# The value projection by seven products, and the order of the linear-attention layer around it

## Chip, cores, metric

The kernel runs on one core of one Trainium2 chip. The metric is device time in microseconds (us) of one execution. Before the change it is 1091.93 us, the median of three runs (1091.86 to 1092.0).

## The reference

Two residual layers over 512 tokens of width 1024: first bidirectional gated linear attention, then softmax attention, each followed by a gated feed-forward block with a width-3 convolution. Only the first half of layer 0 changes here:

```python
def gla_mixer(h, w_in, w_gate_up_f, b_gate_f, w_gate_up_b, b_gate_b, norm_w, w_out):
    proj = h @ w_in
    q, k, v, g, r = jnp.split(proj, ...)
    r_f, r_b = jnp.split(r, 2, axis=-1)
    def log_decay(r_dir, w_up, b_up):
        return heads(jax.nn.log_sigmoid(r_dir @ w_up + b_up) / 16.0, GLA_DK)
    ...
    o_f = gla_chunked(q, k, v, la_f, strict=False)
    o_b = flip(gla_chunked(flip(q), flip(k), flip(v), flip(la_b), strict=True))
    o = rmsnorm((o_f + o_b).transpose(0, 2, 1, 3), norm_w) * jax.nn.silu(g)
    return o.reshape(B, S, GLA_VAL_DIM) @ w_out

x = x + gla_mixer(rmsnorm(x, norm_mix[0]), ...)
```

There are 4 heads with keys of 128 and values of 256; q and k are 512 wide, v and g 1024, r 32. All is float32.

## The kernel before

**Numbers and products.** TensorE takes float32 in a rounded form (`F32R`). Each operand is therefore kept as a high part, the rounded value, and a low part, what the rounding left; a product is three matmuls: high by high, high by low, low by high (`mm3`). A weight tile of 128x1024 is loaded by SP (`raw`), rounded on ScalarE (`wh`) and subtracted on VectorE (`wl`); this is a split (`Weights.split`, L301 to L310). `Weights.low_dma` (L260) makes the low part in another way: ScalarE writes the high part, then the negated high part, and an accumulating DMA on POOL's queue adds the original (`flush`, L298). `Weights` holds a list `todo` of all weight halves in the order of their use, makes them some pieces ahead and asks for loads `LOADS` = 3 ahead. The program's order is a priority: where an instruction isn't ready by the planner's costs, a later one of the same engine is put ahead of it, except where `tc.issue_after` ties it.

**The stage, in order (`gla`).** The tokens are 512, the width is 8 chunks `k` of 128.

1. The input comes as eight 512 KB pieces `xw`, each a chunk of x and the same chunk of the first weights. `norm.chunk` makes `xhl`, the weighted input in two parts.
2. `seg(0)`, `seg(1)` (`token_steps`, L488): v, each half of 512 columns in 4 token blocks x 8 chunks x 3 = 96 matmuls of 128x512. `seg_out` scales a half by the token's inverse norm (`rtok`) and splits it.
3. Beside them: the sums of squares (`norm.square`, L443; `norm.tokens`, `norm.rows`), the rank step `rp` (16 matmuls, L668), its weights and those of the gates, the masks, and `token_sums`, which makes sums of quarters of the input (`xt`) for step 4.
4. `seg_seven`: g by Strassen's scheme in Winograd's form. Tokens, columns and chunks are halved; seven products take the place of eight, each 24 matmuls per half of the weights and product. It needs sums of weight quarters (`make_vg`, four VectorE operations for each of two halves) and the token sums. The seven products are added up in PSUM and in SBUF (L616 to L627).
5. The gates (`gate`, eight: head x direction): a matmul `z`, then absolute value, clamp, exponential, logarithm, a scan over tokens within chunks of 64, and exponentials into `ek` and `fk`. They are begun at set points (`GATE_STEPS`, `LATE_GATES`).
6. Four heads. For each: `kproj`, `qproj` (a key and a query tile, 24 matmuls each), `keys` and `factors` (products with `ek`), `rows` (transposed keys, `kt`, split), `inner` (masked scores `in`; `masked` makes `ath`, `atl`), `outer` (eighteen state matmuls `kv` and twelve on `o`), `outputs` (twelve more on `o` with the states `sa`, `sb`), `gated` (per-token root, times g after silu, copied by DMA into `gr`), `tail` (transposes into `oT`). The projections of the next head stand between the steps of a head.
7. `out_steps`: the output projection, 192 matmuls `op`, added to x, and the next norm's chunks.

The feed-forward of layer 0 follows with the matmuls `up`.

Of the kernel before, what the change touches and what calls it, by code (L numbers as in the profile page):

```python
# [14 lines left out]
P = 128  # L15
# [11 lines left out]
SEG_BANKS = (("acc", "acc", "pt", "pt"), ("s", "s", "acc", "acc"), ("acc", "pt", "pt", "s"), ("s", "acc", "acc", "acc"))  # L27


KQ_DMA = 4  # L30
KQ_AHEAD = 2
BIG_GATES = 9
GATED = 0
WARM = 10
LATE_GATES = {0: (4,), 10: (4,), 30: (4, 5), 40: (5,), 1: (5, 6), 11: (6,), 21: (6,), 31: (7,), 41: (7,), 2: (7,)}
GST_LOW = 0
SEVEN_BANKS = (("pt", "pt"), ("acc", "acc"), ("acc", "s"))
GATE_STEPS = (2, 5, 18, 19, 99, 99, 99, 99)
GATE_LAG = 1
VG_ORDER = (1, 7, 6, 4, 5, 2, 3)  # L40
VG_AHEAD = 3
VG_RAW = {1: (4, "g"), 7: (5, "raw"), 6: (6, "raw"), 2: (7, "raw")}
VG_DMA = ()
SUMS_FIRST = 2
SUMS_AT = {1: 3}
SUMS_MID = (2,)
SUMS_OUT = ()
# [47 lines left out]
def hybrid_encoder_kernel(  # L95
# [9 lines left out]
    w_vg: bass.AP,  # L105
# [50 lines left out]
    def x_save(p):  # L156
        if p == 0:
# [10 lines left out]
    class Weights:  # L168
# [9 lines left out]
        def add(self, src, strips=None, pieces=2):  # L178
            for i in strips or range(src.shape[0]):
# [4 lines left out]
        def load_vg(self, i, half):  # L184
            if i not in VG_RAW or (i, half) in self.vg:
                return
            strip, tag = VG_RAW[i]
            self.vg[i, half] = t = big(F32, "raw") if tag == "g" else pair("raw", NR, F32, "raw")
            sync.dma_start(t, w_vg[strip, :, half * 2 * S : (half + 1) * 2 * S])

        def make_vg(self, i, half):

            self.load_vg(i, half)
            a11, a21, a22, a12 = (self.vg.get((n, half)) for n in (1, 7, 6, 2))
            r = {1: a11, 6: a11, 4: a22, 5: a21, 2: a12, 3: a12}.get(i)
# [9 lines left out]
            if i in VG_DMA:  # L205
                strip = {1: 4, 4: 6, 2: 7}[i]
                self.low_dma(hi, lo, r, w_vg[strip, :, half * 2 * S : (half + 1) * 2 * S].bitcast(F32R))
            else:
                self.split(hi, lo, r)
            return hi, lo  # L210
# [12 lines left out]
        def load(self, key):  # L223
            src, i, h = key
            if i < 0:
                self.load_vg(-i, h)
# [8 lines left out]
        def make(self, key):  # L235
            src, i, h = key
            if i < 0:
                self.made[id(src), i, h] = self.make_vg(-i, h)
# [11 lines left out]
            else:  # L250
                self.split(hi, lo, r, 2 if src is w_vg and i < 2 else 1, src is w_vg and i == 0 and h == 0)
# [99 lines left out]
    W.add(w_vg, range(4))  # L351
    W.todo += [(w_vg, -i, half) for i in VG_ORDER for half in range(2)]
    for a in (w_kq, w_gout):
        W.add(a)
# [16 lines left out]
    for n in range(4):  # L371
        W.loaded[id(w_vg), n // 2, n % 2] = [t[:, S:] for t in raw[2 * n : 2 * n + 2]]
# [115 lines left out]
    def token_steps(src, i0, hl, ps, width, per_half):  # L488

        for hf in range(KC // per_half):  # L490
            wh, wl = W.half(src, i0 + hf)

            late = src is w_vg and i0 > 0 and hf == 0
            for kk in range(per_half):
                todo = [(kk, j, i) for j in range(NT - late) for i in range(3)]
                if late and kk == 1:
                    todo += [(k, NT - 1, i) for k in range(2) for i in range(3)]
                if src is w_vg and i0 + hf * per_half + kk < 2:
                    todo.sort(key=lambda a: a[2])
# [12 lines left out]
    def out_steps(src, hl, nxt, late):  # L512
# [4 lines left out]
        def part(ng, ks):  # L517
            if ng not in pss:
                pss[ng] = [bank("s" if ng % 2 else "acc", "op") for _ in range(2)]
            for k in ks:  # L520
# [4 lines left out]
                for i, (wt, mv) in enumerate(((wh, hl[k][0]), (wh, hl[k][1]), (wl, hl[k][0]))):  # L525
                    for n in range(2):
                        sl = slice((kk * 2 + n) * P, (kk * 2 + n + 1) * P)
                        mm(pss[ng][n], wt[:, sl], mv, start=k == 0 and i == 0, stop=k == KC - 1 and i == 2)  # L528
# [3 lines left out]
        def end(ng):  # L532
# [4 lines left out]
            x_save(ng)  # L537

        for ks in late:
            for ng in range(2):  # L540
                yield from part(ng, ks)
                if KC - 1 in ks:
                    end(ng)
        for ng in (2, 3):
            yield from part(ng, range(KC))
# [3 lines left out]
    def gla(norm, nxt):  # L549
# [7 lines left out]
        v = [(big(F32R, "vh"), None) for _ in range(NT)]  # L557
        q = []

        def seg(i, between=None):  # L560
            ps = [bank(tag, "vg") for tag in SEG_BANKS[i]]
            for n, _ in enumerate(token_steps(w_vg, i * 4, norm.hl, ps, S, 2)):
                if between is not None:
                    between(n)
            return ps

        def seg_out(ps, h):
            for j in range(NT):
                if h == 0:
                    v[j] = v[j][0], pair("x", KC // 2, F32R, "vl")  # L570
                hi, lo = (a[:, h * S : (h + 1) * S] for a in v[j])
                r = norm.rtok[:, j : j + 1]
                act.activation(hi, ps[j], AF.Copy, scale=r)
                dve.scalar_tensor_tensor(lo, ps[j], r, hi.bitcast(F32), ALU.mult, ALU.subtract)
# [984 lines left out]
```

## Time and profile before

| | |
|---|---|
| median of 3 runs | 1091.93 us |
| the profiled execution | 1092.29 us |
| its span, first to last instruction | 1090.6 us |
| granted TensorE clock, mean | 0.999 |
| first matmul of `vg` / first of `up` | 5.84 / 223.75 us |
| HBM read, written | 114.89, 14.68 MB |

In the profile, PE is TensorE, PEld its weight loads, DVE is VectorE, ACT ScalarE, POOL GpSimd, SP the engine whose queue carries the loads. A row of the grouped view reads: line, engine, operation, output<-inputs by the program's names, shapes, count | busy us, mean ns of one | idle time before them and what ended it. A row of the view by stretches has the stretch, its length, then for each engine the busy us and the instructions, the granted clock, the DMA share and GB/s. A row of the timeline has start, length, engine, line, output<-inputs and count. A wait row reads: engine, what waited <- what it waited for: us in total, times, longest. A DMA row ends with the median time from issue to landing. The end of a matmul is modelled; matmuls overlap.

### The profile page before, as it was taken

The page shows a single profiled execution, that of the slowest core. Times are in us where ns is not written, and L with a number is a line of the kernel's source. Part 1 is how long each engine was busy: PE and PEld are TensorE (multiplying, and loading weights), DVE is VectorE, ACT ScalarE, POOL GpSimd, SP SyncE. Part 2 cuts the span into 40 slices and gives each one's busy share as a digit, 9 for nine tenths or more (in the row PEclk, how much of TensorE's full clock was granted, in tenths as well). Part 3 has the DMA queues.
Part 4 walks back from the last instruction along what each step waited for, and adds up shares of the span by engine and source line. Part 5 has one row for each costly group of instructions (what it writes and reads, how often), then busy time and mean ns, then how long its engine had stood idle before and what let it go on. Part 6 is the DMA issues. An engine that isn't in the chain of part 4 may idle for free.

```text
span 1090.6 us, 17422 instructions
## 1 busy us (share of the span) xinstructions
PE 1083.5 (99%) x6696; PEld 971.1 (89%) x6696; DVE 873.4 (80%) x1304; ACT 715.9 (66%) x1120; POOL 136.1 (12%) x153
## 2 busy tenths in 40 slices
PE   9999999999999999999999999999999999999998
PEld 8878888888899999999988888788889999999997
DVE  6886784659898899988855588765989889998882
ACT  8768753469775676666664677646977567665660
POOL 0101222021000100010014343002110010001000
PEclk9999999999999999999999999999999999999999
DMA  9537624488644733265757475558964373226542
GB/s 308 138 116 192 156 97 155 154 186 204 151 117 120 166 115 101 80 158 133 264 131 168 121 215 151 168 173 189 212 138 139 99 167 111 99 87 158 132 174 78
DMA packets 55187, 164.26 MB, mean 151 GB/s; under 512 B 6464, under 2 KB 6976, under 8 KB 55104
## 3 DMA queue, kind: packets, MB, share of 16 engines
q1 hardware_dynamic: 36192, 112.66, 31.3%
q0 software_dynamic: 14016, 41.95, 21.3%
q10 hardware_dynamic: 4896, 8.55, 2.1%
q8 instruction: 52, 0.85, 0.3%
q14 instruction: 31, 0.25, 0.1%
HBM read 114.89 MB, written 14.68 MB: 119 GB/s over the span
## 4 chain that ended last, share of the span: by engine, by line
PE 94%; ACT 3%; DVE 2%; issue 1%; DMA 1%; DVEq 0%; ACTq 0%; SPq 0%
PE r L1035 39%; PE op L528 8%; PE up L470 6%; PE up L471 6%; PE up L472 6%; PE vg L502 3%; PE dn L471 2%; PE dn L470 2%; PE dn L472 2%; PE vg L610 2%; PE av L502 1%; PE o L876 1%; PE A L470 1%; PE A L472 1%; PE B L472 1%; PE B L470 1%
## 5 line engine op out<-in xcount | busy, mean ns | idle before, releaser
L309 ACT ACTIVATE wh<-raw 128x1024 fp32r<-128x1024 f32 x144 | 149.7, 1052 | 73.3 <-PE op L528 22.7
L310 DVE TENSOR_TENSOR wl<-raw,wh 128x1024 fp32r<-128x1024 f32 x144 | 175.2, 1220 | 27.4 <-ACT wh L309 27.2
L1035 PE MATMUL r<-gu,wh 128*128 128x256 f32 x896 | 161.2, 282 | 0.0
L1035 PE MATMUL r<-xt,wh 128*128 128x256 f32 x832 | 150.9, 282 | 0.0
L1035 PEld LDWEIGHTS r<-gu,wh 128*128 128x128 f32 x896 | 139.4, 190 | 1.0 <-ACT r L1172 0.2
L1035 PEld LDWEIGHTS r<-xt,wh 128*128 128x128 f32 x832 | 129.3, 190 | 1.0 <-ACT r L1056 0.5
L1035 PE MATMUL r<-gu,wl 128*128 128x256 f32 x448 | 126.3, 283 | 0.0
L1035 PE MATMUL r<-xt,wl 128*128 128x256 f32 x416 | 117.2, 283 | 0.0
L1035 PE MATMUL r<-nh,wh 128*128 128x256 f32 x312 | 88.7, 284 | 0.0
L1035 PE MATMUL r<-nh,wl 128*128 128x256 f32 x312 | 88.2, 283 | 0.0
L1035 PE MATMUL r<-nl,wh 128*128 128x256 f32 x312 | 87.9, 282 | 0.0
L1035 PEld LDWEIGHTS r<-gu,wl 128*128 128x128 f32 x448 | 85.1, 190 | 0.0
L1035 PEld LDWEIGHTS r<-xt,wl 128*128 128x128 f32 x416 | 79.0, 190 | 0.0
L470 PE MATMUL up<-nh,wh 128*128 128x512 f32 x192 | 75.3, 392 | 0.0
L471 PE MATMUL up<-nl,wh 128*128 128x512 f32 x192 | 75.3, 392 | 0.0
L472 PE MATMUL up<-nh,wl 128*128 128x512 f32 x192 | 75.2, 392 | 0.0
L528 PE MATMUL op<-oT,wh 128*128 128x512 f32 x256 | 71.8, 394 | 0.0
L261 ACT ACTIVATE wh<-raw 128x1024 fp32r<-128x1024 f32 x40 | 42.2, 1055 | 37.0 <-PE up L471 12.1
L1035 PEld LDWEIGHTS r<-nh,wh 128*128 128x128 f32 x312 | 59.3, 190 | 2.5 <-ACT r L1063 2.2
L1035 PEld LDWEIGHTS r<-nl,wh 128*128 128x128 f32 x312 | 59.4, 190 | 0.2
L1035 PEld LDWEIGHTS r<-nh,wl 128*128 128x128 f32 x312 | 59.4, 190 | 0.0
L310 DVE TENSOR_TENSOR wl<-sum,wh 128x1024 fp32r<-128x1024 f32 x44 | 53.6, 1220 | 4.4 <-ACT wh L309 4.4
(290 smaller groups left out, 2768.6 us busy)
## 6 DMA issues: line engine op xcount, KB each, us to landing
raw<-in_w_up_dram SPq DMA_DIRECT2D x84, 512.0 KB, 4.6
raw<-in_w_down_dram SPq DMA_DIRECT2D x44, 512.0 KB, 3.6
wl<-raw POOLq DMA_DIRECT2D x24, 512.0 KB, 5.1
wl<-in_w_up_dram POOLq DMA_DIRECT2D x16, 512.0 KB, 7.7
ring<-p ACTq DMA_DIRECT2D x32, 256.0 KB, 2.8
raw<-in_w_vg_dram SPq DMA_DIRECT2D x12, 512.0 KB, 5.9
xw<-in_xw_dram SPq DMA_DIRECT2D x8, 512.0 KB, 7.0
raw<-in_w_kq_dram SPq DMA_DIRECT2D x8, 512.0 KB, 4.6
```

The source lines that it names most:

```text
L261: act.activation(hi, r, AF.Copy)
L309: act.activation(hi[:, sl], a, AF.Copy)
L310: dve.tensor_tensor(lo[:, sl], a, hi[:, sl].bitcast(F32), ALU.subtract)
L470: mm(ps, wh, mh, start=start, stop=False)
L471: mm(ps, wh, ml, start=False, stop=False)
L472: return mm(ps, wl, mh, start=False, stop=stop)
L502: mm(ps[j][:, :width], hl[k][i == 2][:, j * P : (j + 1) * P], (wl if i == 1 else wh)[:, sl], start=k == 0 and i == 0, stop=k == KC - 1 and ...
L528: mm(pss[ng][n], wt[:, sl], mv, start=k == 0 and i == 0, stop=k == KC - 1 and i == 2)
L610: mm(ps[j], m[:, js], w[:, sl], start=i in (1, 7, 2) and p == 0 and a == 0, stop=i in (4, 2, 3) and p == 3 and a == 2, skip_group_check=True)
L876: last = mm(og[s], l, r, start=False, stop=i == len(parts) - 1, skip_group_check=True)
L1035: mm(dst, w[:, sl], m, start=start and j == 0 and a == 0, stop=j == len(pairs) - 1 and a == 2, skip_group_check=True)
```

## The change

**Order.** The four key/query tiles of heads 0 and 1 take the place of v's first half: they are computed beside the arriving input (`first_tiles`, with the weights as the stationary operand), since `xw` now carries their weights. Then come the key and query of head 2 (`more`, one step of a tile at a time), with rank step and norm beside them, then v by seven products, then the heads; the two tiles of head 3 stand ahead of head 0 and inside head 1 (`FILL_AT`). g by seven products comes behind all heads, the output projection behind g.

**Heads.** `rows` and `inner` of the next head stand ahead of `outputs` of this one. `outputs` copies `o` to SBUF (`O`, two ScalarE copies a head); the squares and roots (`roots`) come in g's stage, and `gated` works on one token block and one half of the columns at a time, as soon as that quarter of g is done. The tails of heads 2 and 3 stand in g's last products, those of heads 0 and 1 behind eight steps of the output projection, which now begins with chunks 4 to 7.

**Weights and sums.** The seven products use another choice of signs, in which every sum of weights is a plain addition; one of four is an accumulating DMA. The token sums of three of four pairs are scaled on VectorE, and three of four low parts are made there. v's quarters need an intermediate tile (`part`), then a high copy and a low difference.

**Gates.** The clamp moves from VectorE to ScalarE (a relu of the negated input) and the addition to an accumulating DMA on POOL's queue.

`PLAN` names the point at which each of these small pieces is issued: f, s, e, v, g for the steps of the first tiles, of head 2's tiles, of head 3's, of v and of g, h for places in the heads.

```diff
-KQ_DMA = 4
-BIG_GATES = 9
-SEVEN_BANKS = (("pt", "pt"), ("acc", "acc"), ("acc", "s"))
+FIRST_BANKS = (("acc", "acc", "pt", "pt"), ("s", "s"))
+SEVEN_BANKS = {"v": (("acc", "acc"), ("pt", "pt"), ("s", "s")), "g": (("acc", "acc"), ("pt", "pt"), ("acc", "po"))}
+BIG_GATES = 4
+MORE = 2
+KQ_DMA = 3
+VG_SUMS = (5,)
+SUM_DMA = (0,)
+SUM_DVE = (0,1,2)
+PLAN = {"f0": ("q5", "q3", "q2", "A1", "s0", "w", "P", "q7", "q4",), "f1": ("q6",), "f2": ("q1",), "f3": ("q0", "s1",), "f4": ("s2", "T",), "f5": ("R",), "f6": ("M",), "first": ("k0", "k2",), "s1": ("k3", "g",), "s6": ("k1", "r",), "s12": ("z1", "s3",), "s13": ("E",), "v1": ("z0",), "v3": ("z1",), "v5": ("z1",), "v6": ("z0",), "v7": ("K0",), "v8": ("z2",), "v13": ("F0", "z3",), "e0": ("z0",), "e4": ("z4", "K1",), "e5": ("z5",), "h0a": ("z4",), "h0b": ("z3", "z5", "z4",), "h0c": ("z3",), "e8": ("z2",), "e15": ("z7", "z2",), "h0d": ("z7",), "h1a": ("K2", "K3", "F1",), "h2a": ("z5", "z6", "z6",), "h3d": ("z6",), "g1": ("S1",), "g2": ("S0",), "g4": ("S3",), "g6": ("S2",), "g11": ("z7",)}
+FILL_AT = (-1,1)
+OUT_FIRST = 8
+TAILS = {"g11": 2, "g12": 3}
...
-            if i == 7:
-                r = pair("raw", NR, F32, "sum")
-                dve.tensor_tensor(r, a21, a11, ALU.subtract)
-            elif i == 6:
-                dve.tensor_tensor(a21, a21, a22, ALU.subtract)
-                dve.tensor_tensor(a11, a11, a21, ALU.subtract)
-            elif i == 3:
-                dve.tensor_tensor(a12, a12, a11, ALU.subtract)
+            plus = {7: a21, 6: a22, 5: a22, 3: a11}.get(i)
+            if plus is not None and i not in VG_SUMS:
+                dve.tensor_tensor(r, r, plus, ALU.add)
...
+            if i in (7, 2) and {7: 5, 2: 3}[i] in VG_SUMS:
+                r, plus = (a21, a22) if i == 7 else (a12, a11)
+                ...
+                self.pending.append((r, plus))
...
+        def more(n, tag):
+            h, i = 2 + n // 2, n % 2
+            ps = bank(tag, "kq")
+            for step, last in enumerate(feature_steps(*W.half(w_kq, n, KQ_AHEAD), norm.hl, ps)):
+                yield last
+            kq_out(h, i, ps)
...
+                if p in SUM_DVE:
+                    dve.tensor_scalar(y[:, i * S : (i + 1) * S], x[2 * p + i], norm.weight(2 * p + i), None, ALU.mult)
+                else:
+                    act.activation(y[:, i * S : (i + 1) * S], x[2 * p + i], AF.Copy, scale=norm.weight(2 * p + i))
...
+            if p in SUM_DMA:
+                W.low_dma(hi, lo, y)
+            else:
+                act.activation(hi, y, AF.Copy)
+                dve.tensor_tensor(lo, y, hi.bitcast(F32), ALU.subtract)
...
-            dve.tensor_scalar(m, z, b, 0.0, ALU.add, ALU.min)
+            act.activation(m, z, AF.Relu, bias=nb, scale=-1.0)
             act.activation(a, a, AF.Exp, scale=-1.0)
             act.activation(a, a, AF.Ln, bias=1.0)
-            dve.tensor_tensor(m, m, a, ALU.subtract)
+            pool.dma_start(m, a, accum_op=ALU.add)
...
+            O[h] = big(F32, "o")
+            for s in (2, 0):
+                act.activation(O[h][:, s * DV : (s + 2) * DV], og[s], AF.Copy)
...
+        def gated(c, o):
+            act.activation(g[c][:, o], g[c][:, o], AF.Silu)
+            for h in ((0, 1) if o.start == 0 else (2, 3)):
+                ...
+                dve.scalar_tensor_tensor(r, O[h][:, cs], ORS[h][:, c : c + 1], r, ALU.mult, ALU.mult)
+                pool.dma_start(gr[h][:, cs].bitcast(F32), r)
...
+        def v_done(c, o):
+            act.activation(v[c][0][:, o], v_part(c, o), AF.Copy)
+            dve.tensor_tensor(v[c][1][:, o], v_part(c, o), v[c][0][:, o].bitcast(F32), ALU.subtract)
...
+        last = seg_seven(w_v, "v", v_part, v_done, v_last)
+        if 0 not in fronts:
+            last = rows(0, last)
+        banks, last = inner(0, last)
+        at = masked(banks)
+        if -1 in FILL_AT:
+            last = fill()
         for h in range(GH):
+            tick(f"h{h}a")
+            st, og, last = outer(h, at, last)
+            tick(f"h{h}b")
+            if h + 1 < GH:
+                keys(h + 1)
+                last = rows(h + 1, last)
+                banks, last = inner(h + 1, last)
+                at = masked(banks)
+            tick(f"h{h}c")
+            if h in FILL_AT:
+                last = fill()
+            last = outputs(h, st, og, last)
+            tick(f"h{h}d")
+        g = [big(F32, "g") for _ in range(NT)]
...
+        seg_seven(w_g, "g", lambda c, o: g[c][:, o], gated, g_last)
...
+        osteps = out_steps(w_gout, oh, nxt, ((4, 5, 6, 7), (0, 1), (2, 3)), (1, 0))
+        for i in range(OUT_FIRST):
             next(osteps)
         sync.dma_start(cw, conv)
+        tail(0)
+        tail(1)
```

The layout of the weights follows: the first two heads' key and query columns go with the input, v and g are each stored as four quarters. `rows(0, last)` also stands inside `seg_seven` at v's step 12 (`ROWS_AT`).

More of the change, by code (lines that the diff above doesn't have):

```diff
@@ L491, in token_steps @@
             wh, wl = W.half(src, i0 + hf)
-            late = src is w_vg and i0 > 0 and hf == 0
             for kk in range(per_half):
[L495 to L499, printed above, removed]
+                todo = [(kk, j, i) for j in range(NT) for i in range(3)]
                 for a, j, i in todo:
@@ L510, in token_tiles, with out_steps @@
             pass
-    def out_steps(src, hl, nxt, late):
+    def out_steps(src, hl, nxt, late, order=(0, 1)):
         pss, ws = {}, {}
@@ L578, in token_sums, with whole @@
+        def whole(steps):
+            for res in steps:
+                pass
+            return res
         def token_sums(p):
@@ L961, in gla @@
-        last = outputs(GH - 1, st, og, last)
-        gated(GH - 1, og)
+        actions = {"q": norm.square, "s": token_sums, "T": lambda _: norm.tokens(), "R": lambda _: norm.rows(),
+                   "w": rank_weights, "g": gate_weights, "P": ranks, "r": rank_rows, "M": masks, "E": table,
+                   "k": lambda n: kq_out(n // 2, n % 2, made["kq"][n]), "z": lambda n: next(gates[n], None),
+                   "K": keys, "F": factors, "S": roots, "A": W.ahead}
+        made["kq"] = first_tiles()
```

483 lines of the change are left out of this document (220 added, 263 removed).

## The prediction

> **What bounds the kernel now.** The page comes first: its span and the line of TensorE.
>
> ```profile
> span 1090.6 us, 17422 instructions
> PE 1083.5 (99%) x6696; PEld 971.1 (89%) x6696; DVE 873.4 (80%) x1304; ACT 715.9 (66%) x1120; POOL 136.1 (12%) x153
> ```
>
> TensorE (PE) is busy for 99% of the span, so a matmul taken out shortens the kernel unless a wait takes its place. The changed stage is the gated linear attention, up to the first up-projection. I cut it at the first matmul of each part: the front (v and g), of it the seven products of g, then the heads, then the output projection.
>
> ```profile
> core 0: us, PE busy (x) PEld busy (x) DVE busy (x) ACT busy (x) POOL busy (x), PEclk, DMA share, GB/s
> 5.84:95.80 89.96, 89.28 (x394) 72.88 (x393) 74.95 (x109) 68.70 (x97) 7.07 (x9) 1.00 0.60 181
> ...
> 55.60:95.80 40.20, 39.52 (x172) 31.67 (x170) 34.12 (x41) 27.15 (x37) 1.72 (x2) 1.00 0.45 131
> 95.80:175.62 79.82, 79.24 (x458) 69.22 (x457) 59.71 (x107) 52.00 (x103) 20.41 (x26) 1.00 0.49 133
> 175.62:223.75 48.13, 48.10 (x223) 39.60 (x221) 24.21 (x37) 19.57 (x33) 5.84 (x10) 1.00 0.53 175
> ```
>
> The granted clock is 1.00 throughout. VectorE (DVE) comes second: 74.95 us busy in the 89.96 us of the front (83%), then 75% in the heads. The waits of TensorE up to 260 us are three:
>
> ```profile
> PE warm L386 <- DVE bd L392: 1.3, 1, 1.3
> PE vg L610 <- DVE wl L310: 0.6, 1, 0.6
> PE o L865 <- DVE atl L828: 0.4, 2, 0.3
> ```
>
> Waits can also hide in matmuls whose modelled ends cover them, so I count starts, not ends. The next rows give the rank step, and the group it belongs to:
>
> ```profile
> 28.30 3.79 PE L668 MATMUL rp<-xhl,rw 128*128 128x512 f32 x16
> 31.92 0.39 PE L502 MATMUL vg<-wh,xhl 128*128 128x512 f32 x1
> ...
> L668 PE MATMUL rp<-xhl,rw 128*128 128x512 f32 x16 | 3.8, 389 | 0.0
> ```
>
> Sixteen matmuls of 512 columns hold TensorE from 28.30 to 31.92, which is 3.62 / 16 = 0.226 us each, although the profile calls one 389 ns long. The price of such a matmul in a full queue is 0.226.
>
> **The matmuls.** These rows count what computes v (L502) and g (L610):
>
> ```profile
> L502 PE MATMUL vg<-wh,xhl 128*128 128x512 f32 x128 | 40.0, 397 | 0.0
> L502 PE MATMUL vg<-wl,xhl 128*128 128x512 f32 x64 | 24.0, 390 | 0.0
> L610 PE MATMUL vg<-wh,xt 128*128 128x512 f32 x64 | 20.2, 392 | 0.0
> L610 PE MATMUL vg<-wh,xhl 128*128 128x512 f32 x48 | 15.4, 389 | 0.0
> L610 PE MATMUL vg<-wl,xt 128*128 128x512 f32 x32 | 12.8, 399 | 0.7 <-DVE wl L310 0.6
> L610 PE MATMUL vg<-wl,xhl 128*128 128x512 f32 x24 | 9.3, 389 | 0.0
> ```
>
> v takes 192, g by seven products 64 + 48 + 32 + 24 = 168. With v by seven too, 24 go: 24 x 0.226 = 5.42 us. The key and query tiles (192 matmuls), rank step, gates, transposes, states and output projection keep their counts; they only move. This is the main term: **-5.4 us**.
>
> [...]
>
> **The new stage lengths.** The front (up to the end of v) loses 96 matmuls of v's second half's plain form against 48 of head 2's two tiles, since v's 168 stand where g's stood: 89.96 - 48 x 0.226 = 79.1 us, and 0.7 for head 0's transposes makes 79.8, with the stalls of before in it. The heads lose the six key/query tiles that now stand ahead of v: 79.82 - 144 x 0.226 - 0.7 = 46.6. The new block of g is 168 x 0.226 = 38.0; the output projection stays 48.1. So VectorE and ScalarE get 10 us less in the front and 33 less in the heads. Whether they keep up decides what is left of the 5.4.
>
> **VectorE in the front.** The durations:
>
> ```profile
> L310 DVE TENSOR_TENSOR wl<-raw,wh 128x1024 fp32r<-128x1024 f32 x26 | 31.5, 1221 | 10.4 <-ACT wh L309 10.4
> L698 DVE TENSOR_TENSOR gm<-gm,ga 128x512 f32<-128x512 f32 x8 | 6.8, 844 | 5.4 <-ACT ga L697 5.3
> L695 DVE TENSOR_SCALAR gm<-z,prm 128x512 f32<-128x512 f32 x8 | 6.0, 747 | 2.2 <-ACT ga L694 1.9
> L627 DVE SCALAR_TENSOR_TENSOR g<-vg,rtok,g 128x512 f32<-128x512 f32 x6 | 4.2, 746 | 0.1
> L802 DVE TENSOR_TENSOR ktl<-kt,kth 128x384 fp32r<-128x384 f32 x8 | 4.2, 546 | 0.0
> L828 DVE TENSOR_TENSOR atl<-at,ath 128x512 fp32r<-128x512 f32 x4 | 2.8, 691 | 0.0
> L890 DVE SCALAR_TENSOR_TENSOR g<-o,ors,g 128x256 f32<-128x256 f32 x16 | 6.6, 478 | 3.5 <-POOL ors L404 3.5
> ```
>
> and, from another part of the kernel, the nearest row of a scaled copy between buffers:
>
> ```profile
> L1389 DVE TENSOR_SCALAR p<-p,rc x32: 471/478/2282, 610.5 to 701.1; 128x512 f32<-128x512 f32 x32
> ```
>
> What goes: four splits of v's plain second half (4 x 1.22 = 4.9); two of eight weight sums of the same 128x1024 form (2.4), since one of four per half of the weights becomes an accumulating DMA; the clamps and additions of the four gates begun there, now ScalarE's and the DMA's (4 x 0.75 + 3 x 0.84 = 5.5), and a third gate's scan and fixing (1.9, by a 1.22 scan and half-width rows near 0.42). Evacuation: eight products of v at 0.75 and seven of g at 0.75 become six accumulations (0.746), six low halves (0.69) and two last ones (0.75): -1.1. Together -15.8. What comes: six scalings of keys and queries (6 x 0.69 = 4.1); six scaled copies for the token sums, a form that before shows on this engine only as L1389 (6 x 0.48 = 2.9; bounds 0.48 and, by L695, 0.75); three low halves of those sums that were DMAs (3 x 1.22 = 3.7); head 0's keys and factors (4 x 0.70) and transposed low halves (2 x 0.55), 3.9. Together +14.6. VectorE's 74.95 becomes 73.8 of 79.8 us, or **92%**, up from 83%.
>
> I cost this at nothing because of a stretch of the feed-forward behind:
>
> ```profile
> 240.00:285.00 45.00, 45.00 (x199) 37.06 (x198) 44.52 (x77) 41.62 (x53) 9.62 (x11) 1.00 0.88 192
> ```
>
> VectorE is busy 44.52 of 45.00 there, and TensorE 45.00. ScalarE loses six scalings, three low halves and four splits and gains the gates' clamps, so it stays near its 76% (68.70 of 89.96). The cover is thin all the same. The first product with token sums of g shows it at 61 to 72 us, where starts slip by 1.6 us: 40.20 for 168 x 0.226 = 38.0 and two gate matmuls (0.45); the wait of 0.6 on `wl` above is part of it. There are two such sets now. v's meets a fuller VectorE, g's comes behind the heads with loads and sums in hand. Each can cost 0 to 1.7; I take 2.1 for both, **+0.5** on before.
>
> **The heads.** Their VectorE work of 59.71 us loses, by the same rows and the counts in that window, six scalings (4.1), head 0's part (3.9), the gating of three heads (12 x 0.48 = 5.8), four splits of output weights (4.9), four clamps and five additions of gates (7.2), a fifth gate's scan (1.9) and four tail halves (4 x 0.75 = 3.0): 30.8. It gains g's first four splits and two sums (7.3) and v's last parts (4.4): 40.6 of 46.6, or 87%. Throughput suffices. What is exposed is the chain behind the masked scores: copy, predicated copy, high half, low half, then `o`. Two of the four heads have no projection tile behind it any more. Before shows one head with a tile behind its inner products:
>
> ```profile
> 128.23 1.95 PE L815 MATMUL in<-ek 128*128 128x128 f32 x16
> 129.93 0.48 PE L470 MATMUL k<-xhl,wh 128*128 128x512 f32 x1
> ```
>
> ```profile
> 137.88 0.69 DVE L828 TENSOR_TENSOR atl<-at,ath 128x512 fp32r<-128x512 f32 x1
> ```
>
> and the last head, which has none, from the `outputs` of the head before (L876) to its own first products (L865):
>
> ```profile
> 167.48 0.60 PE L876 MATMUL o<-sb,ek 128*128 128x256 f32 x2
> ...
> 170.07 1.95 PE L815 MATMUL in<-ek 128*128 128x128 f32 x16
> 171.78 0.36 PE L470 MATMUL kv<-vh,kth 128*128 128x256 f32 x1
> ...
> 173.98 0.28 PE L865 MATMUL o<-vh,ath 128*128 128x256 f32 x1
> ...
> 174.22 0.28 PE L865 MATMUL o<-vh,ath 128*128 128x256 f32 x1
> 174.45 0.39 PE L865 MATMUL o<-vh,atl 128*128 128x256 f32 x1
> ```
>
> In the bare head the product with `atl` starts 0.23 behind its neighbour instead of 0.12 (half of 173.98 to 174.22): a slip of 0.1. The change puts twelve `outputs` (167.48 to 170.07, 2.6 us) behind the inner products, ahead of the eighteen state products (171.78 to 173.98, 2.2 us), and the gating of the head before has left. I take **+0.5** for two bare heads; bounds 0 and 4 (a rival below). The gating moves behind g: silu, sixteen products and the DMAs of the far half come 5 us ahead of the first tail, and two heads' tails stand behind eight output steps of 6 x 0.226 = 1.36 us, so their 11 us hide it.
>
> **Queues.** POOL issues four kq transfers and three sums' transfers less, eight for the gates and four for the weights more, and is 12% busy. A gate's addition, 0.84 us on VectorE, becomes a 256 KB accumulation:
>
> ```profile
> gr<-g POOLq DMA_DIRECT2D x16, 128.0 KB, 2.2
> xd<-f POOLq DMA_DIRECT2D x16, 256.0 KB, 4.0
> wl<-raw POOLq DMA_DIRECT2D x24, 512.0 KB, 5.1
> ```
>
> I take 4.0 us, bounds 2.2 and 5.1. The scan behind it is late by some 3 us, and then that head's exponentials and keys; each gate begins a head or more ahead of its keys, so this is nothing on the path. The sum of weights by DMA (5.1) has two products, 48 x 0.226 = 10.8 us, before it is read. SP carries the same weights in another order.
>
> **Sum.** -5.4 + 0.5 + 0.5 = **-4.4 us**. The profiled execution took 1092.29 us around its span of 1090.6; its span becomes 1086.2, its time 1087.9. It lay 0.36 above the median 1091.93, so the forecast is **1087.5 us**.
>
> **The rivals.**
>
> *The old slips go too.* Set 1.6 us of slips in g's first products and 0.8 in the heads to zero, since both sets find weights ready: -5.4 - 1.6 - 0.8 = -7.8, 1084.1 us. For it: the silu with two table loads leaves the middle of the heads. Against: v's set has less slack than g's had.
>
> *The heads' chain takes the gain.* In the filled head `atl` began 137.88 - 129.93 = 8.0 us behind the inner products, its steps queued behind gates and splits, and took 0.7. The new cover is 2.6 + 2.2 = 4.8 us, which makes a slip of 3.9 in head 1, whose neighbours are the gates of heads 2 and 3. -5.4 + 3.9 + 0.5 = -1.0: 1090.9, within the noise. Late accumulations lead here too, by delaying keys. [...]
>
> *VectorE binds the front (slower).* If VectorE can't be busier there than the 83.3% of before, because its low halves wait for ScalarE's high ones (10.4 us idle in the L310 row), the front takes 73.8 / 0.833 = 88.6 us instead of 79.8: +8.8 - 5.4 + 0.5 = +3.9, 1095.8. It decides against the change from 79.8 + 5.4 = 85.2 us on, below 86.6%. Against it stands the 99% at 240 to 285, though there the weights' splits make most of the work.
>
> *The change doesn't do what it says* would leave 192 matmuls for v; the code has one loop for both, so I give it nothing.
>
> **How the numbers follow.** A measurement tells some 0.2%, 2.2 us, from no change: faster is below 1089.7, slower above 1094.1. Forecast, 1085.4 to 1089.7: 0.50. Old slips gone: 0.14. Heads' chain, 1089.7 to 1094.1: 0.18. VectorE binding: 0.18, of which a half ends below 1095. So faster 0.64, same 0.18, slower 0.18. The range runs from 1083.4, a little under the first rival, to 1094.0; it leaves out most of the last case and a little of the first. The likeliest case alone spans 1085.4 to 1089.7.
>
> **What would show it.** Right: 168 matmuls for each of v and g, 24 fewer in all, and `up` first at some 219.3 us instead of 223.75; VectorE above 90% up to 85 us with under 2 us of slips; `atl` less than 5 us after `in` in heads 1 and 3. Wrong: TensorE waiting for `wl`, `xt` or `v`'s high half for more than 5 us before the heads, for `atl`, `kth` or keys for 4 or more within them, or a first output step that waits for `oT`.

## The result and the profile after

The changed kernel takes 1089.35 us (median; 1088.49 to 1090.18) against 1092.25 for the kernel before beside it (1091.58 to 1093.41): a ratio of the means of 0.9972 [0.9963, 0.9981], which is 3.1 us less, interval 2.1 to 4.0. The forecast was 4.4 less. The 1087.5 us forecast were 1.9 too low; 1089.35 lies in the range of 1083.4 to 1094.0 and, near its upper end, in the likeliest case of 1085.4 to 1089.7. The page after:

```profile
span 1087.5 us, 17403 instructions
PE 1078.5 (99%) x6672; PEld 966.8 (89%) x6672; DVE 885.4 (81%) x1319; ACT 723.3 (67%) x1137; POOL 142.2 (13%) x158
```

24 matmuls fewer; the span is 3.1 shorter. Cut at the same kinds of places as before, by windows (front; heads, first and second part; g; output projection up to the first `up`):

```profile
core 0: us, PE busy (x) PEld busy (x) DVE busy (x) ACT busy (x) POOL busy (x), PEclk, DMA share, GB/s
5.63:84.70 79.07, 78.67 (x353) 64.88 (x353) 73.36 (x117) 61.54 (x89) 12.49 (x15) 1.00 0.77 214
84.70:112.60 27.90, 25.04 (x162) 21.52 (x160) 23.25 (x42) 23.48 (x48) 8.81 (x10) 1.00 0.34 67
112.60:135.20 22.60, 22.60 (x143) 20.71 (x143) 19.70 (x34) 15.11 (x39) 5.20 (x5) 1.00 0.53 129
135.20:175.10 39.90, 39.90 (x186) 33.01 (x185) 27.29 (x38) 28.09 (x47) 9.51 (x15) 1.00 0.48 159
175.10:220.40 45.30, 45.30 (x210) 37.28 (x209) 27.25 (x38) 20.57 (x28) 3.36 (x6) 1.00 0.53 172
```

`up` starts at 220.4 instead of 223.75: 3.35 us of the gain is made before it, and the 867 us behind it are as long as they were (1087.5 - 220.4 = 867.1; before, 1090.6 - 223.75 = 866.9). Nearly all of TensorE's idle time lies in one stretch, the first part of the heads: 25.04 busy of 27.90. Its waits after:

```profile
PE kv L477 <- ACT ga L736: 1.0, 1, 1.0
PE o L875 <- ACT o L890: 0.5, 1, 0.5
PE o L875 <- DVE at L835: 0.5, 1, 0.5
PE kt L803 <- POOL end L784: 0.5, 1, 0.5
PE vg L647 <- DVE wl L315: 0.4, 1, 0.4
PE in L821 <- DVE vl L948: 0.3, 1, 0.3
```

Before had two such rows, 0.6 and 0.4 in all. After has six, each with a releaser of its own, and five of them lie between 86 and 111 us.

Counting starts, as the prediction did, gives the whole account. I call slip what lies between two starts beyond what that shape takes in a full queue, by the starts in the changed kernel's trace (0.227 us for 512 columns, 0.12 for 256 columns of split operands, 0.216 for 256 columns where they aren't split):

| us of slip, up to `up` | before | after | change forecast | change measured |
|---|---|---|---|---|
| first token-sum sets of v and g | 1.6 | 0.9 | +0.5 | -0.7 |
| heads | 2.1 | 5.3 | +0.5 | +3.2 |
| output projection | 0.4 | 0.1 | 0 | -0.3 |
| the rest (start, norm) | 1.0 | 0.9 | 0 | -0.1 |
| total | 5.1 | 7.2 | +1.0 | +2.1 |

24 x 0.227 = 5.45 taken out and 2.1 put back make the 3.35. The step that is off is the heads.

### The profile page after: what moved, and what is told of

Its sections match the earlier page's. It is cut to its first block, busy times and chain, and to the rows that moved or that the text cites. A ratio compares the mean times of both kernels' runs of the same rounds, so it can differ in the third digit from the quotient of the medians.

```text
span 1087.5 us, 17403 instructions
## 1 busy us (share of the span) xinstructions
PE 1078.5 (99%) x6672; PEld 966.8 (89%) x6672; DVE 885.4 (81%) x1319; ACT 723.3 (67%) x1137; POOL 142.2 (13%) x158
## 4 chain that ended last, share of the span: by engine, by line
PE 94%; DVE 2%; ACT 2%; DMA 1%; issue 0%; POOL 0%; DVEq 0%; ACTq 0%; POOLq 0%
PE r L1060 37%; PE op L530 8%; PE vg L647 6%; PE up L477 6%; PE up L478 6%; PE up L479 6%; PE kq L579 2%; PE dn L477 2%; PE dn L478 2%; PE dn L479 2%; PE av L504 1%; PE A L477 1%; PE A L479 1%; PE B L477 1%; PE A L478 1%; PE B L479 1%
## 5 line engine op out<-in xcount | busy, mean ns | idle before, releaser
L315 DVE TENSOR_TENSOR wl<-raw,wh 128x1024 fp32r<-128x1024 f32 x156 | 189.8, 1219 | 31.8 <-ACT wh L314 31.4
L314 ACT ACTIVATE wh<-raw 128x1024 fp32r<-128x1024 f32 x156 | 162.8, 1053 | 64.7 <-PE op L530 21.7
L1060 PEld LDWEIGHTS r<-gu,wl 128*128 128x128 f32 x448 | 85.1, 190 | 0.0
L266 ACT ACTIVATE wh<-raw 128x1024 fp32r<-128x1024 f32 x36 | 38.0, 1056 | 37.0 <-PE up L478 12.1
L530 PEld LDWEIGHTS op<-oT,wh 128*128 128x128 f32 x256 | 47.4, 188 | 9.8 <-ACT oT L923 0.3
```

What stands on the lines that cost most here:

```text
L266: act.activation(hi, r, AF.Copy)
L314: act.activation(hi[:, sl], a, AF.Copy)
L315: dve.tensor_tensor(lo[:, sl], a, hi[:, sl].bitcast(F32), ALU.subtract)
L530: mm(pss[ng][n], wt[:, sl], mv, start=k == late[0][0] and i == 0, stop=k == late[-1][-1] and i == 2)
L1060: mm(dst, w[:, sl], m, start=start and j == 0 and a == 0, stop=j == len(pairs) - 1 and a == 2, skip_group_check=True)
```

## What the experiments were to tell apart

Four theories of the 3.2 us in the heads and of what would come next:

- **A, the gates' transfer.** The addition is an accumulating DMA; its scan, exponentials and keys come late by its latency.
- **B, missing cover.** Bare heads have no projection tile behind their inner products.
- **C, VectorE's work.** VectorE, 93% busy in the front, is the bound there, and what is added to it or taken from it shows in the time.
- **D, the mass of gate work.** Five of the eight gates run between 84.7 and 112.6, and it is their work on ScalarE and VectorE that stands in the way.

One caution holds for all single profiles: the first matmuls run slower than later ones, by an amount that differs between the profiles. Four of 512 columns take 0.91 us in a full queue (4 x 0.227); the first four take 1.04 us in fill_in_head0 (5.46 to 6.50) and up to 1.87 in gate3_earlier (5.63 to 7.50). The rank step starts at 22.0 us in the changed kernel's profile and at 21.0 to 22.1 in the others, with the same work ahead of it. So stages below are counted from that start. Behind `up` single profiles differ by up to 3.2 us (866.7 to 869.8) with the same matmuls in the same order, so the medians judge the whole.

All stages in one table, from the starts in each trace: from the rank step's first matmul to the first matmul behind head 0's inner products, from there to g, from g to `up`. Rounded figures can miss their sum by 0.1. gates_without_add, gates_clamp_only, v_24_fewer, v_no_sums and the kernels made of these leave work out; they are there to find causes, not as faster kernels.

| kernel | front | heads | g, output | sum | median us | ratio to before |
|---|---|---|---|---|---|---|
| changed kernel | 65.0 | 48.3 | 85.2 | 198.4 | 1089.35 | 0.9972 [0.9963, 0.9981] |
| gates2_add_on_dve | 66.5 | 49.0 | 86.3 | 201.8 | 1093.53 | 1.0014 [1.0005, 1.0023] |
| gates_without_add | 65.1 | 47.0 | 85.9 | 198.1 | 1088.56 | 0.9971 [0.9959, 0.9984] |
| gate3_add_on_dve | 65.1 | 47.9 | 85.1 | 198.1 | 1089.73 | 0.9976 [0.9966, 0.9986] |
| gate3_earlier | 69.0 | 57.2 | 85.1 | 211.3 | 1101.32 | 1.0081 [1.0066, 1.0096] |
| fill_in_head0 | 65.5 | 53.1 | 85.1 | 203.7 | 1094.90 | 1.0027 [1.0018, 1.0037] |
| all_sums_on_dve | 67.4 | 53.2 | 85.5 | 206.1 | 1096.22 | 1.0038 [1.0023, 1.0053] |
| sums_scaled_on_act | 66.3 | 48.4 | 85.2 | 199.9 | 1090.59 | 0.9989 [0.9979, 0.9998] |
| v_24_fewer | 65.8 | 52.3 | 85.2 | 203.2 | 1096.37 | 1.0037 [1.0025, 1.0050] |
| v_no_sums | 64.4 | 48.2 | 85.1 | 197.8 | 1087.80 | 0.9963 [0.9948, 0.9978] |
| v_no_sums_24_fewer | 62.7 | 49.0 | 85.4 | 197.1 | 1089.18 | 0.9971 [0.9960, 0.9981] |
| gates_clamp_only | 65.0 | 48.1 | 85.2 | 198.3 | 1088.50 | 0.9968 [0.9957, 0.9979] |
| v_no_sums_gates_clamp_only | 64.4 | 48.1 | 86.0 | 198.5 | 1088.79 | 0.9967 [0.9954, 0.9979] |

The last column of stages hardly moves. Everything is decided in the front and the heads.

A second caution: an edit can also shift the order in which TensorE's instructions are put. Only gates_without_add, gate3_add_on_dve and v_no_sums have the changed kernel's order in full. In the four kernels whose heads take over 52 us (gate3_earlier, fill_in_head0, all_sums_on_dve, v_24_fewer) one or two transposes of head 2's later keys (`kt`) stand ahead of the twelve state products behind which the changed kernel has them, and one of these waits 2.0 to 3.4 us for POOL's keys. In all the others no `kt` waits longer than 0.7. So, by these waits, the loss in the heads of those four is in good part the price of this order, and of the lower clock behind such a wait (0.85 and 0.92 from 112.6 to 135.2 us in gate3_earlier and v_24_fewer; for all_sums_on_dve there is the mean of its profile alone, 0.997 against 0.999 in the changed kernel's; last section); it can't be read as the price of the work that was moved. No run has their edit in the old order.

## The experiments on the gates' addition (A)

**gates2_add_on_dve.** The addition of gates 2 to 7 goes back to VectorE.

```diff
-            pool.dma_start(m, a, accum_op=ALU.add)
+            if n >= 2:
+                dve.tensor_tensor(m, m, a, ALU.add)
+            else:
+                pool.dma_start(m, a, accum_op=ALU.add)
```

> The addition of the six gates from the third on goes back from the accumulating DMA to VectorE; the first two, which fall into the front, keep the DMA. Theory A (the DMA makes the gates of the first heads late, and with them ScalarE's queue, the bank that gates and states share, and the transposed keys): VectorE's waits for a gate's DMA (4.7 us in the changed kernel) go, the slips of TensorE between 84.7 and 112.6 us fall from about 6 us to 3 or less, and the kernel is 2 to 4 us faster than the changed one. Theory B (the heads are short of cover by projection tiles, whatever the gates do): slips stay within 1 us, time within 1 us. Theory C (VectorE is the bound): six additions of 0.69 more make it up to 4 us slower.

It is 4.2 us slower than the changed kernel. Front 1.5 longer, heads 0.8, and g 1.1, where transposes wait for the gated outputs' transfers. Theory A's gain does not appear; the direction is C's. But the order of matmuls shifted too, so the next two keep it.

**gates_without_add** leaves the addition of those gates out, **gate3_add_on_dve** moves that of gate 3 alone. Both have the changed kernel's order on TensorE.

```diff
-            pool.dma_start(m, a, accum_op=ALU.add)
+            if n < 2:
+                pool.dma_start(m, a, accum_op=ALU.add)
```

> The addition of the logarithm in the gates from the third on is left out, so there is neither a transfer nor an operation of VectorE between logarithm and scan; the order of TensorE's instructions is the same as in the changed kernel. Theory A (the gates' transfers, 2.5 to 3 us each, make the heads' keys and the bank shared by gates and states late): the slips between 84.7 and 112.6 us fall from about 5.5 to 3 or less, and the kernel is 2 to 4 us faster than the changed one (ratio to before about 0.994 to 0.996). Theory D (VectorE and ScalarE are full there by the mass of work: gates 3 to 7 beside heads 0 and 1; a transfer costs nothing): slips stay within 1 us, ratio 0.9965 to 0.998.

> One gate, the fourth (second direction of head 1), has its addition on VectorE, where VectorE waited 2.8 us for the transfer at 93 us; TensorE's order is unchanged. Theory A: that wait goes, the slip of 1.2 us at 96 us goes with it, and 1 to 2 us are gained on the changed kernel. Theory D: VectorE has 0.7 us more to do, no gain, up to 1 us lost.

Each reaches `up` 0.3 us sooner, counted from the rank step, and neither median can be told from the changed kernel's. Without the six transfers the wait of `kv` on the relu falls from 1.17 us of slip to 0.21, but new ones appear; the waits of that kernel from 20 to 228 us:

```profile
PE kt L804 <- POOL end L785: 0.7, 1, 0.7
PE vg L647 <- DVE wl L315: 0.5, 1, 0.5
PE in L822 <- DVE sa L865: 0.5, 1, 0.5
...
```

So the transfers cost the kernel a few tenths, not the 3.2 (the heads alone get 1.2 shorter, but g gets 0.8 longer). They are shorter than the 4.0 taken, by the changed kernel's rows of DMA issues (the last figure is the median from issue to landing, us):

```profile
gm<-ga POOLq DMA_DIRECT2D x4, 256.0 KB, 3.4
ga<-ga POOLq DMA_DIRECT2D x4, 256.0 KB, 3.3
```

**gate3_earlier** begins gate 3 three steps earlier in v, which by A should bring its keys sooner.

```diff
-"v13": ("F0", "z3",)
+"v10": ("z3",), "v13": ("F0",)
```

> The fourth gate begins at v's step 10 in place of 13, some 7 us earlier. Theory A and a late start as its cause: keys of head 1 are ready before they are needed, the 1.2 us at 96 us go, 1 to 2 us gained. Theory D: its 4.7 us of VectorE and ScalarE work stands in v then, where VectorE is busy 94%: head 0's inner products end 1 to 3 us later, no gain.

It is 12 us slower, 4.0 of it in the front. The timeline of the front's end, in excerpts, shows how an accumulation can hurt after all:

```profile
84.70 1.05 PE L821 MATMUL in<-ek 128*128 128x128 f32 x8
86.91 1.22 DVE L748 TENSOR_TENSOR_SCAN ga<-gconst,gm 128x512 f32<-128x512 f32 x1 [3.90 <-DMA gm<-ga]
90.24 1.40 DVE L948 SCALAR_TENSOR_TENSOR vl<-vg,rtok,vh 128x512 fp32r<-128x512 f32 x2
91.04 0.79 PE L477 MATMUL kq<-xhl,wh 128*128 128x512 f32 x1 [2.57 <-DVE vl L948]
...
92.06 0.63 PE L479 MATMUL kq<-xhl,wl 128*128 128x512 f32 x1
92.48 0.63 PE L477 MATMUL kq<-xhl,wh 128*128 128x512 f32 x1
```

The scan stands in VectorE's queue ahead of other work and waits 3.90 us for the transfer, which took 6.5 us here (80.35 to 86.88) against 3.3 in the changed kernel. Behind it stands `vl`, the evacuation of v's last bank, and TensorE waits for that. In the changed kernel gate 3's scan waits too, 2.8 us at 93, in the heads, and there gates_without_add shows that it costs little. So A has a true mechanism, and its price hangs on what is queued behind the scan. The heads' 8.9 us are another matter: `kt`, out of its old place, waits 3.3 there.

## The experiment on the cover (B)

**fill_in_head0** moves the second tile of head 3 from inside head 1 to inside head 0.

```diff
-FILL_AT = (-1,1)
+FILL_AT = (-1,0)
```

> Head 3's query tile moves from inside head 1 to inside head 0, so that the masked scores of head 1 have a tile of 5.4 us behind them and those of head 2 have none. Theory B (missing cover in head 1): the two slips at its products with the masked scores, 0.7 and 0.7 us, go, and 1 to 2 us are gained; head 2's stay under 0.5. Theory A (late gates): the tile gives the gates 5.4 us more, too, so the gain is also 1 to 3 us, but the wait of 1.2 us at 96 us, which lies ahead of the tile, stays as it is in either.

The heads take 4.8 us longer. The wait of `o` on `at`'s low half is gone, as B had it, but `kt` waits 2.0 for POOL's `end` and `o` 1.7 for the copies of O, so the slips moved to neighbours and grew. And the changed kernel itself speaks against B: from 118.1 on, where the last tile is done, head 3 runs with no projection tile behind its inner products, as head 1 does, and TensorE is busy all the time (22.60 of 22.60 us from 112.6 to 135.2). The tile's place matters, a tile's absence alone doesn't.

## The experiments on VectorE (C)

**all_sums_on_dve** puts the sums of weights that are made by DMA on VectorE too, **sums_scaled_on_act** the scaling of the token sums on ScalarE.

```diff
-VG_SUMS = (5,)
+VG_SUMS = ()
```

> The one sum of weights of four that went by accumulating DMA is made on VectorE, for v and for g: four more operations of 1.22 us, two of them in the front. If TensorE sets the pace: the same as the changed kernel within 1 us. If VectorE is the bound of the front: 2 to 3 us slower, as waits for low parts of weights before 84 us.

```diff
-SUM_DVE = (0,1,2)
+SUM_DVE = ()
```

> The six scalings of the token sums go from VectorE back to ScalarE: VectorE has 6 x 0.48 = 2.9 us less in the front, ScalarE 4.3 more. If VectorE binds the front, as 24 matmuls fewer in v without any gain say, the inner products of head 0 end 1 to 3 us earlier than at 87.0 us and v's slips shrink. If the front hangs on something else (ScalarE, loads), they end at 87.0 or later, by up to 2 us.

The first costs 6.9 us. In its profile 2.5 lie in the front, in which VectorE got two more sums (2.4 us) and ScalarE waits 2.9 for the last of them, and 4.9 in the heads, where `kt`, out of its old place, waits 3.4 for POOL. The second takes 2.8 us off VectorE (six copies of 0.487) and is 1.2 slower: ScalarE is late with the first tiles, and a new wait stands there:

```profile
PE kq L479 <- DMA wl<-raw: 1.6, 1, 1.6
```

From then on VectorE only catches up, 39.92 busy of the 40.20 us from 44.5 to 84.7.

**v_24_fewer** leaves out 24 matmuls more in v; **v_no_sums** leaves out the six additions of v's weights on VectorE (7.3 us) and keeps TensorE's order; **v_no_sums_24_fewer** does both. They ask which engine sets the front's end.

```diff
+                                if name == "v" and i in (1, 6, 5) and a == 2:
+                                    continue
```

```diff
-            if plus is not None and i not in VG_SUMS:
+            if plus is not None and i not in VG_SUMS and src is w_g:
```

> In three of v's seven products (the first, the third and the fifth) the matmuls of the low input parts are left out, 24 of 512 columns; all splits and sums are still made. Prediction's price (0.226 us each, TensorE sets the pace of the front): 5.4 us less than the changed kernel, slips in v under 1.5 us. VectorE binds the front (it is busy 94% of v's stage already): less than 2.7 us of the 5.4 is gained, and slips of more than 2.5 us appear where TensorE waits for the weights' low parts.

> The six additions of weight quarters in v's stage are left out (VectorE 6 x 1.2 = 7 us less in the front); TensorE's instructions and their order are those of the changed kernel. VectorE carries the front without holding TensorE up by more than the 1.2 us of slips before 87 us: head 0's inner products end at 85.8 to 87 us, VectorE is busy 68 to 69 us up to there in place of 75.7, ratio to before 0.9955 to 0.997.

> As above, and the 24 matmuls of low input parts left out as well. If VectorE was what kept the 24 from showing in the front (75.6 us busy by the same time in both kernels), they show now: head 0's inner products end near 82 us, 4 to 5.4 us ahead of the kernel that has only the sums left out. If something else held it (loads, ScalarE, a fixed wait of the first head), they end at 86 or later again.

The front is 0.8 longer with 24 matmuls fewer, 0.6 shorter without the sums (the slip at v's first token sums, no more), and 2.2 shorter with both, between the two outcomes that were expected. The timeline of v_24_fewer at its end, in excerpts:

```profile
81.32 1.05 PE L823 MATMUL in<-ek 128*128 128x128 f32 x8
82.82 1.02 DVE L808 TENSOR_TENSOR ktl<-kt,kth 128x384 fp32r<-128x384 f32 x2 [0.41 <-ACT kth L807]
84.14 1.23 DVE L315 TENSOR_TENSOR wl<-raw,wh 128x1024 fp32r<-128x1024 f32 x1 [0.30 <-ACT wh L314]
85.15 0.60 ACT L830 ACTIVATE at<-in 128x512 f32<-128x512 f32 x1
85.28 1.41 DVE L950 SCALAR_TENSOR_TENSOR vl<-vg,rtok,vh 128x512 fp32r<-128x512 f32 x2
85.81 2.07 PE L823 MATMUL in<-ek 128*128 128x128 f32 x8 [3.43 <-ACT at L830]
```

and of the changed kernel:

```profile
84.70 1.05 PE L821 MATMUL in<-ek 128*128 128x128 f32 x8
85.25 1.41 DVE L948 SCALAR_TENSOR_TENSOR vl<-vg,rtok,vh 128x512 fp32r<-128x512 f32 x2
86.05 1.16 PE L821 MATMUL in<-ek 128*128 128x128 f32 x8 [0.30 <-DVE vl L948]
```

In the changed kernel the second half of head 0's inner products waits for a bank that VectorE empties with `vl`. With 24 matmuls fewer TensorE is there 3.4 us sooner, but `vl` starts at 85.28 instead of 85.25, and the wait, 3.43 us now, ends with ScalarE's copy of the first half, `at`. VectorE began the delay and ScalarE carries it on, by the waits of ScalarE in v_24_fewer:

```profile
ACT wh L314 <- DVE raw L201: 3.3, 2, 2.7
```

The longer of the two, for VectorE's last sum of v, ends at 76.51, and from there on ScalarE is busy without a pause (6.00 of 6.00 us from 78 to 84), with `at` at the end of its queue. TensorE also waits 2.2 us for `wl` within v (0.4 in the changed kernel). So in the changed kernel TensorE and the two engines arrive together, to 0.3 us: VectorE, and ScalarE's queue behind it, bind the front from here on, and fewer matmuls in v alone are worth nothing. With the sums gone as well `vl` starts at 82.06, still 3.7 behind the inner products at 78.40: the scan of a gate has held VectorE's queue for 2.0 us, until its transfer landed at 76.9, and the low half of v before, the keys' low halves and a split of g's first weights stand behind it and ahead of `vl`. That is a matter of order, and another order wasn't tried. The heads of v_24_fewer are 4.0 longer: `kt`, out of its old place, waits 3.5 us for POOL's keys in them, and the granted clock is 0.73 from 84.7 to 91.0 us, where the wait of 3.43 ends, and 0.92 from 112.6 to 135.2 (the last section).

## The experiments on the gates' mass (D)

**gates_clamp_only** keeps of gates 3 to 7 the clamp alone, ahead of the scan; the last kernel does that and v_no_sums together.

```diff
-            act.activation(a, z, AF.Abs, bias=b)
+            if n < 3:
+                act.activation(a, z, AF.Abs, bias=b)
```

> The absolute value, exponential, logarithm and addition of the gates from the fourth on are left out: ScalarE has 5 x 1.9 = 9.6 us less beside heads 0 and 1, and the gates are shorter by the same steps and the transfer. Theory D (mass of gate work beside heads 0 and 1, ScalarE and VectorE 84% busy between 84.7 and 112.6 us): the slips there fall from about 5.5 to 2.5 us or less, and the span is 2.5 to 4 us below the changed kernel's. If the slips come from the heads' own chain (bare heads, one bank for gates and states, order), they stay above 4.

> Both: without the sums in v and with the shortened gates, what VectorE and ScalarE take from the 5.4 us is given back. Slips up to the first up-projection fall from 7.3 to under 4 us, the first up-projection starts at 217 us or earlier (220.4 in the changed kernel), ratio to before 0.993 to 0.9955.

Three ScalarE operations of 0.64 to 0.69 us and a transfer less for each of five gates, some 10 us of ScalarE, and the heads take 48.1 instead of 48.3. The slips from 84.6 to 112.3 sum to 5.0. D falls, as far as this kernel can tell: it isn't the amount of work. (Its order on TensorE shifted in heads 0 and 1, so slips could also have come anew with the order.) The last kernel was to reach `up` at 217 us or earlier and does so at 220.5, with the heads at 48.1. The waits of gates_clamp_only from 20 to 228 us are again of the old size with other releasers (here L737 is the relu, L786 the keys on POOL):

```profile
PE kv L477 <- ACT ga L737: 1.3, 2, 1.0
PE kv L477 <- DVE kq L590: 0.9, 1, 0.9
PE kt L805 <- POOL end L786: 0.7, 1, 0.7
```

## Why the prediction was right, and where it was off

**The matmuls: right.** v and g share one line now, and its counts halve to 168 each (128 + 96 + 64 + 48 = 336):

```profile
L647 PE MATMUL vg<-wh,xt 128*128 128x512 f32 x128 | 39.9, 389 | 0.0
L647 PE MATMUL vg<-wh,xhl 128*128 128x512 f32 x96 | 31.1, 395 | 0.0
L647 PE MATMUL vg<-wl,xt 128*128 128x512 f32 x64 | 25.0, 391 | 0.4 <-DVE wl L315 0.4
L647 PE MATMUL vg<-wl,xhl 128*128 128x512 f32 x48 | 18.9, 393 | 0.0
```

The price of 0.226 each holds: full queues of 512 columns show 0.226 to 0.227 in the changed kernel too. That 5.45 less 2.1 of slips makes the 3.35 measured is no second proof, since a slip is what goes beyond this price.

**The front: right.** 79.8 us were forecast and 79.07 came; VectorE 73.8 and 73.36, so 93% against 92%. The rival in which VectorE can't be busier than 83% is out. Still, v_24_fewer shows that the margin was nil: the fuller VectorE, costed at nothing, cost a wait of 0.3 us at the front's end, and a matmul less in v would have gained nothing.

**The two sets: too dear.** +0.5 was taken, -0.7 came. v's set slips 0.67, g's 0.2.

**The heads: the mis-sized term.** "I take +0.5 for two bare heads; bounds 0 and 4." The mechanism was named and the measured +3.2 lies within the bounds, but it isn't a matter of bare heads. The slips lie in heads 0 and 1, the four largest 1.17, 0.70, 0.69 and 0.65 us. The first, in excerpts of the timeline:

```profile
94.78 0.21 ACT L761 ACTIVATE fk<-fk 128x3 f32<-128x3 f32 x1 [0.80 <-DVE fk L754]
95.12 0.63 ACT L759 ACTIVATE ek<-ga 128x512 f32<-128x512 f32 x1
...
95.66 0.61 ACT L760 ACTIVATE ek<-ga 128x512 f32<-128x512 f32 x1
96.18 0.67 ACT L736 ACTIVATE ga<-z,gconst 128x512 f32<-128x512 f32 x1
96.90 0.38 PE L477 MATMUL kv<-vh,kth 128*128 128x256 f32 x1 [1.00 <-ACT ga L736]
```

The state products share a bank (`po`) with a gate's `z`. Its second reader is the clamp, which the change moved to ScalarE, and there it stands behind two exponentials of another gate. These were late themselves: in the row of `fk` ScalarE stands idle for 0.80 us, for gate 3's scan on VectorE, which had waited 2.8 us for its transfer. So the slip has two causes in a row; without the transfers it is 0.21 (A). The prediction counted the clamp's time on each engine and not the bank that it holds. The chain behind the masked scores in head 1, which it did price, in excerpts:

```profile
103.56 0.75 DVE L831 COPY_PREDICATED at<-smask,in 128x512 f32<-128x512 uint8 x1
104.34 0.63 ACT L834 ACTIVATE at<-at 128x512 fp32r<-128x512 f32 x1
104.70 0.28 PE L479 MATMUL kv<-vh,ktl 128*128 128x256 f32 x1
104.88 1.07 ACT L890 ACTIVATE o<-o 128x512 f32<-128x512 f32 x2
105.51 0.39 PE L875 MATMUL o<-vh,at 128*128 128x256 f32 x1 [0.54 <-ACT o L890]
105.80 0.69 DVE L835 TENSOR_TENSOR at<-at,at 128x512 fp32r<-128x512 f32 x1
106.54 0.50 PE L875 MATMUL o<-vh,at 128*128 128x256 f32 x2 [0.53 <-DVE at L835]
```

`at`'s low half starts 4.5 us behind the end of the inner products (101.3). The prediction counted 4.8 us of cover, with eighteen state products in it; only six of them stand here (the last at 104.70), so the first product on `o` could have started 3.5 us behind the inner products. The products of head 1 lose 1.4 us in all, 0.70 of it in a wait that ends with the copies of O and 0.69 in one that ends with `at`'s low half. In head 3 the low half starts 2.2 us behind the inner products, and nothing is lost. So the rival of the heads' chain was the right mechanism at a third of its price at most (1.4 of 3.9), joined by three waits of the same size that the prediction didn't price: the bank, the copies and the keys on POOL.

The stage lengths behind the front were added up wrongly. The last head's `outputs` (2.4 us) stood behind 175.62 and were counted to the output projection, and sixteen transposes of two tails (1.8 us) moved from the heads into g, which the forecast of 46.6 for the heads and 38.0 for g left out. With both, and 3.2 of slips, the heads' 50.5 (84.70 to 135.20) and g's 39.9 come out. The sum doesn't feel it.

**Luck in the sum.** The heads came 2.7 us dearer than they were taken, the two sets 1.2 cheaper, the rest 0.4. That the sum is off by 1.1 and not by 2.7 is luck.

**What stays open.** Taking away the transfers, the abs, exponential and logarithm, or sums on VectorE each removed or shrank one wait and left the heads within 1.2 us of 48.3. By the waits, the 3.2 us come from several short in-order chains that follow each other closely, but no kernel got them back, so this is read from the traces and not shown by a run; how much each would give alone, above all a bank of its own for `z`, wasn't tried. And no kernel that computes all of it was faster than the changed one.

## What to carry to other kernels

When a matmul is taken out, ask which buffer its successor waits for and which engine empties it: a second engine at 93% can be in step to a few tenths, and then the next saving on TensorE is worth nothing. When an operation moves to another engine, price the buffer that it reads as well as its time, since its place in the new queue decides when the buffer comes free. Before a time is put down to an edit, compare the order of the instructions in the two traces: a shifted order can cost more than the edit. In a stage of short dependent steps count the chains that end on TensorE, and put a price on each, not on the one that looks longest.

## Not expected of the hardware

**A pause can be paid twice.** Behind the wait of 3.4 us in v_no_sums_24_fewer nine matmuls of 512 columns take from 84.58 to 88.57, 3.99 us instead of 9 x 0.227 = 2.04; in gate3_earlier, after waits of 1.55 and 2.57 us, eleven take from 91.04 to 95.90, 4.86 instead of 2.50. Behind the first of them the spacing is 0.427 us. The granted clock (the column before the DMA share) shows it; windows of v_no_sums_24_fewer, and one of fill_in_head0, where a wait of 1.97 us ends at 115.64:

```profile
78.00:84.00 6.00, 2.59 (x16) 2.33 (x15) 5.93 (x12) 5.30 (x9) 0.00 (x0) 0.82 0.46 91
84.70:91.00 6.30, 6.30 (x22) 5.02 (x21) 3.42 (x5) 1.84 (x5) 1.71 (x2) 0.69 0.24 42
91.00:97.00 6.00, 6.00 (x44) 5.27 (x43) 3.89 (x8) 5.82 (x14) 1.90 (x3) 1.00 0.25 44
...
117.60:119.00 1.40, 1.40 (x9) 1.40 (x8) 1.36 (x7) 1.07 (x4) 0.06 (x1) 0.50 0.62 108
```

The changed kernel's waits of up to 1.0 us leave the clock at 1.00, and so does one of 1.56 in sums_scaled_on_act. The spacing of 0.427 us in place of 0.227 and the clock of 0.50 in fill_in_head0 agree. The longest single wait ahead of the slow stretch is 3.41 us in v_no_sums_24_fewer, 2.57 in gate3_earlier and 1.97 in fill_in_head0, with shorter ones near the last two. How long a pause must be to lower the clock these runs don't show.

**The start differs by up to 1 us.** In fill_in_head0 no two of the first matmuls of 512 columns start 0.42 us or more apart; in the changed kernel the first three steps are at 0.43 to 0.59 us. From the first of them to the rank step it takes 15.6 us there and 16.4 here. With the first one's own start (5.46 and 5.62) this moves everything behind by up to 1 us and can pass for an effect of an edit.
